# Set-up spread over more points, early evictions, pools of their own, last block by halves, in a hybrid decoder step

## The chip, the cores and the metric

The kernel runs on one NeuronCore of a Trainium2 chip. The metric is device microseconds of one execution, taken as the median of the runs. In profile rows PE is the matmul engine (PEld its weight loads), DVE the vector engine, ACT the scalar engine, POOL the GpSimd engine and SP the queue that issues most transfers. PSUM is the accumulator memory that PE writes, SBUF the working memory.

## What is computed

One step of a two-layer decoder trunk in float32 on 512 prompt tokens and 64 sample tokens (8 sequences of 8), model width 1024, feed-forward width 2816. Layer 0 mixes tokens by dilated attention (three groups, 8 heads of 64), layer 1 by a complex diagonal state-space model (64 groups of 16 channels, 64 states each). Each is followed by a SwiGLU feed-forward.

```python
def attention_layer(h, pos, bufs, w_qkv, q_gain, k_gain, w_o):
    qkv = (h @ w_qkv).reshape(B, T, 3, N_DIL, N_HEAD_SLOTS, HEAD_DIM)
    q = rope(rmsnorm(qkv[:, :, 0], q_gain), pos)
    k = rope(rmsnorm(qkv[:, :, 1], k_gain), pos)
...
    return o @ w_o, new_bufs

def ssm_layer(h, state0, w_in, a_re, a_im, log_dt, b_re, b_im, c_re, c_im, d_skip, w_glu):
    u = (h @ w_in)
    dt = jnp.exp(log_dt)[:, None]
    abar = jnp.exp(lam * dt)
    bbar = ((abar - 1.0) / lam)[..., None] * bmat
...

def swiglu(h, w_gate, w_up, w_down):
    return (jax.nn.silu(h @ w_gate) * (h @ w_up)) @ w_down

def trunk(x, pos, attn_bufs, ssm_states, p):
    for i in range(DEPTH):
        h = rmsnorm(x, p['norm_mix'][i])
...
        x = x + out
        x = x + swiglu(rmsnorm(x, p['norm_ffn'][i]), ...)
```

Besides the two outputs it returns the new key and value caches and the new state.

## The kernel before

The program runs through the phases in order: `qkv_phase`, `attn_phase`, `wo_phase` (attention's output product and residual), `ffn` of layer 0, `ssm_phase`, `ffn` of layer 1. From `wo_phase` on, all activations lie transposed, feature by token, in `xT` (8 tiles of 128 features by NT = 576 tokens, two halves of HN = 288). A tile framework inserts the semaphores and orders the instructions of each engine by its own estimate, except those that are kept in program order (`Kept`, `tc.keep_in_program_order`) or held behind another with `tc.issue_after`. A tile from a pool waits until the last user of its buffer is done; a pool that closes gives its memory to later pools, whose first users then wait for the last users of the old one.

Every large product takes both operands as a high and a low part and adds three products: `split_w` makes the parts of a weight load (512 KB `raw` from HBM, ACT copies `whi`, DVE subtracts for `wlo`, each with two buffers), `split` those of an activation, and `mm6` issues six matmuls of 288 columns.

**QKV.** `qkv_chunk` makes 512 columns of Q, K or V at a time, nine chunks (`CHUNKS`), each in four quarters `kk` of the contraction over five row tiles `t` of tokens, in five PSUM buffers. Between the quarters a queue of slots runs score products, rotations and transposes of earlier chunks; the order is kept. After the chunk `qk_chunk` or the V variant empties the accumulators on ACT into tiles `a`; the next chunk starts in the buffer of `t = 0`.

**Attention and output.** `attn_phase` writes its result to `att`. In `wo_phase`, `ath` is the high part of `att` (ACT), `atl` the low part (DVE); `xr0` to `xr3` are the quarters of the residual, loaded back from HBM and added to the products by DVE. Three accumulators `acc0` to `acc2`, two banks each, are used in turn; the first of them lie on the banks of attention.

**Feed-forward and set-up.** `ffn` goes over the inner width in three parts (`THIRDS`). For each 256 columns there are two weight loads for the gate and two for the up product, 48 matmuls for each load (four contraction tiles, two 128-wide row tiles `m`, six matmuls); the down product follows in four blocks `c`. DVE multiplies the gate accumulator (`gt`), ACT takes silu, POOL multiplies, DVE makes `ut` with the up accumulator and the split of the result (`hh`, `hl`). In layer 0 a generator, `ssm_setup`, is advanced by `step()` after each inner tile and each down block, 34 times; it computes the constants of the state-space layer. Its last loop runs over eight rounds `f`: DVE makes the products `wr`, PE transposes them into `aux`, ACT copies them to `wo`; DVE fills `cb` from `Cr` and `Cn`, PE multiplies `wr` by `cb`, DVE copies to `kk`, PE transposes `kk`, DVE copies that to `kt`, spreads it with eight shuffles into `st` and masks it (stored as T); POOL makes six products for V, in the buffers of `wr` and `wt`. In layer 1 the last third's blocks are transposed back by PE (`aux`), copied by ACT to `yo` and by DVE to `ys`, and stored (`o_yp` from SP, `o_ys` from ACT).

Of the kernel before, what the change touches and what calls it, by code (L numbers as in the profile page):

```python
# [50 lines left out]
def _build(nc, tc, A, es):  # L51
# [50 lines left out]

    def mm6(ps, wh, wl, xh, xl, first, last):
        for i, (w, x) in enumerate(((wh, xh), (wh, xl), (wl, xh))):
            for c in range(2):
                te.matmul(ps[:, c, :HN], w, x[:, c * HN:(c + 1) * HN], start=first and i == 0, stop=last and i == 2)  # L106
# [16 lines left out]
    with ExitStack() as qs:  # L123
# [24 lines left out]
        rs_.close()  # L148
# [4 lines left out]
    accp = es.enter_context(tc.tile_pool(name="acc2", bufs=1, space=PSUM))  # L153
    turn = [0]

    def acc(i=None):
        if i is None:
            i = turn[0] % 3
            turn[0] += 1
        return accp.tile([128, 2, 512], F32, name=f"acc{i}")  # L160
# [261 lines left out]
def qkv_phase(nc, tc, A, es, L):  # L422
# [233 lines left out]
    def v_chunk(gi, wk, vt=None, order=range(5), then=None):  # L656
# [93 lines left out]
def attn_phase(nc, tc, A, es, L):  # L750
# [7 lines left out]
    kp = es.enter_context(pool("kpa", bufs=4))  # L758
# [169 lines left out]
    values(15, dec[7].out)  # L928
    return wo, raws[1]


def wo_phase(nc, tc, A, es, L):
    v, s, g, te = nc.vector, nc.scalar, nc.gpsimd, nc.tensor
    pool, xT, att, fetch_w, split_w, mm6, acc, n0 = (L[x] for x in ("pool", "xT", "att", "fetch_w", "split_w", "mm6", "acc", "n0"))
    wk = es.enter_context(pool("wko"))
    xr = []
    for c in range(4):
        xr.append(wk.tile([128, 2, NT], F32, name=f"xr{c}"))
        nc.sync.dma_start(xr[c], L["xscr"][:, 2 * c:2 * c + 2])
    ath = wk.tile([128, 4, NT], F32R, name="ath")  # L940
    atl = wk.tile([128, 4, NT], F32R, name="atl")
    kv_, ks = Kept(tc, v), Kept(tc, s)
    for k in range(4):
        ks.activation(ath[:, k], att[:, k], AF.Copy)
# [24 lines left out]
    return last  # L969
# [5 lines left out]
def ffn(nc, tc, A, L, layer, nin, nout, fill):  # L975
# [4 lines left out]
    def step():  # L980
# [3 lines left out]
    def gemm(src, width, ks, c0, xs, first=True, last=True):  # L984
        ps = [acc() for _ in range(2)]
        for a in range(0, len(ks), 4):
            n = min(4, len(ks) - a)
            wh, wl = load_w(src, width, ks[a], n, c0, 256)
            for m in range(2):
                for k in range(n):  # L990
                    xh, xl = xs[ks[a + k]]
                    mm6(ps[m], wh[:, k, m * 128:(m + 1) * 128], wl[:, k, m * 128:(m + 1) * 128], xh, xl, a + k == 0, a + k == len(ks) - 1)
        return ps

    with ExitStack() as es:
        hp = es.enter_context(pool("hp", bufs=9))
        wk = es.enter_context(pool("wkf", bufs=2))
        for c0, c1 in THIRDS:
            h = {}
            for c in range(c0, c1):  # L1000
# [9 lines left out]
                for m in range(2):  # L1010
# [3 lines left out]
                    step()  # L1014
# [555 lines left out]
```

## Time and profile before

| | before |
|---|---|
| median of 3 runs | 1504.01 us (1503.43 to 1505.36) |
| profiled execution | 1506.59 us |
| its span, granted clock | 1504.8 us, 0.999 |
| PE / DVE / ACT / POOL busy | 98% / 60% / 35% / 21% |

The span is the time between the first and last instruction of the profiled execution. A row of the timeline gives start and duration in microseconds, engine, line, operation, output and inputs, shape and count; in brackets stands the idle time of that engine just before and what ended it. A row of the waits gives who waited for whom: total, times and longest. A row of a group gives the line, what it does, its count, busy time, mean nanoseconds of one and idle time ahead. In a row by windows, busy microseconds and counts of PE, PEld, DVE, ACT and POOL follow the length of the window.

### The profile page before, as it was taken

The page shows a single profiled execution, that of the slowest core. Times are in us where ns is not written, and L with a number is a line of the kernel's source. Part 1 is how long each engine was busy: PE and PEld are TensorE (multiplying, and loading weights), DVE is VectorE, ACT ScalarE, POOL GpSimd, SP SyncE. Part 2 cuts the span into 40 slices and gives each one's busy share as a digit, 9 for nine tenths or more (in the row PEclk, how much of TensorE's full clock was granted, in tenths as well). Part 3 has the DMA queues.
Part 4 walks back from the last instruction along what each step waited for, and adds up shares of the span by engine and source line. Part 5 has one row for each costly group of instructions (what it writes and reads, how often), then busy time and mean ns, then how long its engine had stood idle before and what let it go on. Part 6 is the DMA issues. An engine that isn't in the chain of part 4 may idle for free. (4 is left out here: it accounts for less than half of the span.)

```text
span 1504.8 us, 29545 instructions
## 1 busy us (share of the span) xinstructions
PE 1471.7 (98%) x12406; PEld 1382.3 (92%) x12406; DVE 909.9 (60%) x1507; ACT 526.1 (35%) x814; POOL 322.3 (21%) x377
## 2 busy tenths in 40 slices
PE   9999999999899999999999999999999999999998
PEld 7878777777799999999999999899999999999998
DVE  5898988745468653789778568745443333333332
ACT  4534455464552222222122454433432222221222
POOL 2022231320040138345345220211111001100100
PEclk9999999999999999999999999999999999999999
DMA  7566788989875555987667748864555555442212
GB/s 245 208 228 234 236 287 264 359 299 348 243 240 196 196 198 183 310 275 256 238 215 260 280 124 254 251 218 157 194 196 195 222 194 195 137 137 84 84 64 71
DMA packets 191253, 322.64 MB, mean 214 GB/s; under 512 B 39984, under 2 KB 137520, under 8 KB 189712
## 3 DMA queue, kind: packets, MB, share of 16 engines
q1 hardware_dynamic: 182960, 303.24, 59.5%
q10 hardware_dynamic: 4992, 10.04, 2.0%
q0 software_dynamic: 3168, 7.48, 1.4%
q8 instruction: 97, 1.59, 0.4%
q14 instruction: 36, 0.29, 0.1%
HBM read 289.22 MB, written 118.78 MB: 271 GB/s over the span
## 5 line engine op out<-in xcount | busy, mean ns | idle before, releaser
L106 PE MATMUL acc<-xgl,whi 128*128 128x288 f32 x1760 | 379.3, 296 | 1.0 <-DVE xgl L173 1.0
L106 PE MATMUL acc<-xgh,wlo 128*128 128x288 f32 x1760 | 377.3, 295 | 0.0
L106 PE MATMUL acc<-xgh,whi 128*128 128x288 f32 x1760 | 377.2, 296 | 0.1
L100 DVE TENSOR_TENSOR wlo<-raw,whi 128x1024 fp32r<-128x1024 f32 (+1 forms) x166 | 205.3, 1237 | 238.6 <-ACT whi L99 235.4
L99 ACT ACTIVATE whi<-raw 128x1024 fp32r<-128x1024 f32 (+1 forms) x166 | 172.4, 1039 | 461.1 <-PE acc L106 409.6
L106 PEld LDWEIGHTS acc<-xgl,whi 128*128 128x128 f32 x1760 | 282.7, 188 | 2.5 <-DVE xgl L173 1.3
L106 PEld LDWEIGHTS acc<-xgh,wlo 128*128 128x128 f32 x1760 | 283.0, 188 | 0.6 <-issue 0.2
L106 PEld LDWEIGHTS acc<-xgh,whi 128*128 128x128 f32 x1760 | 281.6, 188 | 0.5 <-DVE gt L1005 0.3
L1007 POOL TENSOR_TENSOR gt<-gt,rstd 128x576 f32<-128x576 f32 x44 | 77.2, 1756 | 430.6 <-ACT gt L1006 430.5
L106 PE MATMUL acc<-hh,whi 128*128 128x288 f32 x704 | 151.3, 296 | 0.0
L106 PE MATMUL acc<-hh,wlo 128*128 128x288 f32 x704 | 151.3, 295 | 0.0
L106 PE MATMUL acc<-hl,whi 128*128 128x288 f32 x704 | 151.0, 295 | 0.0
L338 PE MATMUL acc<-whi,xh 128*128 128x512 f32 x288 | 118.9, 414 | 3.7 <-ACT a L747 2.0
L106 PEld LDWEIGHTS acc<-hl,whi 128*128 128x128 f32 x704 | 113.1, 188 | 0.2 <-issue 0.2
L106 PEld LDWEIGHTS acc<-hh,wlo 128*128 128x128 f32 x704 | 113.1, 188 | 0.2 <-issue 0.2
L106 PEld LDWEIGHTS acc<-hh,whi 128*128 128x128 f32 x704 | 113.1, 188 | 0.0
L338 PE MATMUL acc<-wlo,xh 128*128 128x512 f32 x288 | 112.2, 391 | 0.0
L338 PE MATMUL acc<-whi,xl 128*128 128x512 f32 x288 | 111.5, 393 | 0.0
L193 POOL TENSOR_TENSOR ssum<-ssum,sq 128x576 f32<-128x576 f32 x21 | 36.2, 1723 | 159.2 <-ACT sq L192 159.2
L338 PEld LDWEIGHTS acc<-whi,xh 128*128 128x128 f32 x288 | 54.0, 188 | 14.5 <-ACT a L747 2.7
L1019 DVE TENSOR_TENSOR xT<-acc,xT 128x576 f32<-128x576 f32 x48 | 36.3, 757 | 49.2 <-PE acc L106 49.2
L1006 ACT ACTIVATE gt<-gt 128x576 f32<-128x576 f32 x44 | 30.2, 686 | 100.2 <-DVE gt L1005 94.5
(389 smaller groups left out, 2047.5 us busy)
## 6 DMA issues: line engine op xcount, KB each, us to landing
o_kv_s<-cache_kv_w SPq DMA_DIRECT2D x64, 1020.0 KB, 7.1
kc<-cache_kv_w SPq DMA_DIRECT2D x100, 512.0 KB, 7.1
raw<-ffn_w_gate SPq DMA_DIRECT2D x44, 512.0 KB, 3.9
raw<-ffn_w_up SPq DMA_DIRECT2D x44, 512.0 KB, 3.8
raw<-ffn_w_down SPq DMA_DIRECT2D x40, 512.0 KB, 3.5
raw<-w_qkv SPq DMA_DIRECT2D x36, 512.0 KB, 7.0
kc<-qscr SPq DMA_DIRECT2D x32, 512.0 KB, 6.2
o_kv_s<-cache_kv_w SPq DMA_DIRECT2D x16, 1008.0 KB, 5.8
```

Source lines behind the costliest of these rows:

```text
L99: s.activation(hi, raw, AF.Copy)
L100: mark[0] = v.tensor_tensor(lo, raw, hi.bitcast(F32), OP.subtract)
L106: te.matmul(ps[:, c, :HN], w, x[:, c * HN:(c + 1) * HN], start=first and i == 0, stop=last and i == 2)
L193: g.tensor_tensor(self.ss, self.ss, sq, OP.add)
L338: ins = nc.tensor.matmul(*a, **kw)
L1006: s.activation(t, t, AF.Silu)
L1007: g.tensor_tensor(t, t, nin.r, OP.mult)
L1019: v.tensor_tensor(xv, ps[m][:, :, :HN], xv, OP.add)
```

## The change

All five parts keep the arithmetic; PE has the same matmuls, and one more store is issued each from ACT and from SP. The changed kernel's file is longer, so its line numbers are higher.

**1. Projections.** The accumulators of row tiles 0 and 1 of every chunk but the first are emptied right after their last matmul, inside the chunk's last quarter:

```diff
-        ps = qkv_chunk(nc, L, x, begin, step, x.prep if first else None, None if first else slot)
-        at = [wk.tile([128, 512], F32, name="a", bufs=6) for _ in range(5)]
-        for t in range(4):
-            s.activation(at[t], ps[t], AF.Copy, scale=x.rc[:, t:t + 1])
+        def ends(ps, t):
+            if t < 2:
+                at.append(wk.tile([128, 512], F32, name="a", bufs=6))
+                s.activation(at[t], ps[t], AF.Copy, scale=x.rc[:, t:t + 1])
+
+        ps = qkv_chunk(nc, L, x, begin, step, x.prep if first else None, None if first else slot, range(5), None if first else ends)
...
-            ps = qkv_chunk(nc, L, x, begin, step, None, slot)
-            for t in range(5):
+            ps = qkv_chunk(nc, L, x, begin, step, None, slot, range(5), lambda ps, t: ends(ps, t) if t < 2 else None)
+            for t in range(2, 5):
```

ACT's rows at the end of the last chunk of K, before (`kT` and `ks` are copies of transposes, `Sall` of scores, `a<-acc` the evictions):

```order
L747 ACTIVATE kT_94<-pt 128x4x128
L747 ACTIVATE ks<-pt 128x512
L747 ACTIVATE Sall<-Sd 128x136
L747 ACTIVATE kT_94<-pt 128x4x128
L747 ACTIVATE Sall<-Sd 128x136
L747 ACTIVATE a<-acc,rr 128x512 x4
L747 ACTIVATE ks<-acc,rr 64x512
L747 ACTIVATE whi<-raw 128x1024
```

and after:

```order
L760 ACTIVATE kT_94<-pt 128x4x128
L760 ACTIVATE Sall<-Sd 128x136
L760 ACTIVATE a<-acc,rr 128x512
L760 ACTIVATE ks<-pt 128x512
L760 ACTIVATE a<-acc,rr 128x512
L760 ACTIVATE kT_94<-pt 128x4x128
L760 ACTIVATE ks<-pt 128x512
L760 ACTIVATE Sall<-Sd 128x136
L760 ACTIVATE kT_94<-pt 128x4x128
L760 ACTIVATE Sall<-Sd 128x136
L760 ACTIVATE a<-acc,rr 128x512 x2
L760 ACTIVATE ks<-acc,rr 64x512
```

Two of the four evictions moved ahead of the chunk's last copies of `ks`, `kT` and `Sall`.

**2. Attention's output.** `ath` gets a pool of its own on the other side of memory and is filled in `attn_phase`, its rows 0 to 2 ahead of the last products; the products of the first block are reordered, so that row 3 comes last. The three accumulators get PSUM pools of their own.

```diff
     dec[7].values(1)
-    values(15, dec[7].out)
-    return wo, raws[1]
+    ek.close()
+    ath = L["rs_"].enter_context(L["right"]("wath")).tile([128, 4, NT], F32R, name="ath")
+
+    def between():
+        dec[7].out()
+        for k in range(3):
+            s.activation(ath[:, k], att[:, k], AF.Copy)
+
+    values(15, between)
+    s.activation(ath[:, 3], att[:, 3], AF.Copy)
+    return wo, raws[1], ath
...
-                for m, k in ((m, k) for m in range(2) for k in range(4)) if x is atl else ((m, k) for k in range(4) for m in range(2)):
+                for m, k in ((0, 0), (0, 1), (0, 2), (1, 0), (1, 1), (1, 2), (0, 3), (1, 3)) if x is ath else ((m, k) for m in range(2) for k in range(4)):
...
-    accp = es.enter_context(tc.tile_pool(name="acc2", bufs=1, space=PSUM))
+    accp = [es.enter_context(tc.tile_pool(name=f"acc2{i}", bufs=1, space=PSUM)) for i in range(3)]
```

**3. Residual quarters.** Each quarter has a pool of its own and its load is kept in program order; the ten small loads of `ssm_setup` are held behind the last of them.

```diff
-        xr.append(wk.tile([128, 2, NT], F32, name=f"xr{c}"))
-        nc.sync.dma_start(xr[c], L["xscr"][:, 2 * c:2 * c + 2])
+        xr.append(es.enter_context(pool(f"wko{c}")).tile([128, 2, NT], F32, name=f"xr{c}"))
+        xl = tc.keep_in_program_order(nc.sync.dma_start(xr[c], L["xscr"][:, 2 * c:2 * c + 2]))
...
-        nc.sync.dma_start(tmask, A["c_tm"])
+        with tc.issue_after(L["xload"].ins):
+            nc.sync.dma_start(tmask, A["c_tm"])
```

SP's queue from the weight load ahead of them, before:

```order
L87 DMA raw<-ffn_w_gate 128x4x256
L1120 DMA raw<-ssm_a_re 32x128
L1121 DMA raw<-ssm_a_im 32x128
L1123 DMA ldt<-ssm_log_dt 32x2
L1127 DMA cw<-ssm_c_re 128x8x64
L1128 DMA cw<-ssm_c_im 128x8x64
L1130 DMA bw<-ssm_b_re 128x32x16
L1131 DMA bw<-ssm_b_im 128x32x16
L939 DMA xr_5039<-x_scr 128x1152
L939 DMA xr_5041<-x_scr 128x1152
L939 DMA xr_5043<-x_scr 128x1152
L939 DMA xr_5045<-x_scr 128x1152
```

and after:

```order
L87 DMA raw<-ffn_w_gate 128x4x256
L961 DMA xr_5049<-x_scr 128x1152
L961 DMA xr_5054<-x_scr 128x1152
L961 DMA xr_5059<-x_scr 128x1152
L961 DMA xr_5064<-x_scr 128x1152
L1110 DMA tmask<-c_tm 128x8
L1113 DMA dcol<-ssm_d 128x8x1
L1117 DMA dmask<-c_dm 128x16
L1159 DMA raw<-ssm_a_re 32x128
L1161 DMA raw<-ssm_a_im 32x128
L1164 DMA ldt<-ssm_log_dt 32x2
L1169 DMA cw<-ssm_c_re 128x8x64
```

The four `xr` loads moved ahead of seven loads of the set-up; the three others (`tmask`, `dcol`, `dmask`) followed them before and still do, and all of `cw` and `bw` follow.

**4. The set-up.** `tick()` takes the place of `step()`, after every weight load's matmuls (68 times instead of 34), and the generator has about twice as many yields. A round of its last loop now takes four ticks: transposes of `wr`; products; transpose of `kk`, shuffles and `powers(f + 1)`, which are DVE's products and `cb` copies of the next round; mask and V. PE's part is held behind the last matmul so far, and V is made in the buffer `st`.

```diff
+            tick()
         return ps
...
+            def powers(f):
...
+                wr[f] = wk.tile([128, 2, 4, 16, 8], F32, name="wr")
+                wt = wk.tile([128, 2, 4, 16, 8], F32, name="wt")
+                cmul(v, wr[f][:, 0], wr[f][:, 1], bw_(Br), bw_(Bi), rv(Ar), rv(Ai), wt[:, 0], wt[:, 1])
                 for i, c in ((0, Cr), (1, Cn)):
                     for gl in range(2):
                         hs = slice(gl * 64, gl * 64 + 64)
                         v.tensor_copy(cb[i][hs, :, gl, :], c[hs, qs, :])
+
+            powers(0)
+            yield
+            yield
+            for f in range(8):
+                ps = aux.tile([128, 2, 512], F32, name="aux")
+                with tc.issue_after(L["pem"][0].ins):
...
+                s.activation(wo.rearrange("p r q c -> p r (q c)"), ps, AF.Copy)
+                nc.sync.dma_start(scn["W"][f], wo)
+                yield
+                pk = aux.tile([128, 2, 512], F32, name="aux")
+                with tc.issue_after(L["pem"][0].ins):
...
+                v.tensor_copy(kk, pk[:, 0, :128])
+                v.scalar_tensor_tensor(k7, dmask, dcol[:, f:f + 1], k7, op0=OP.mult, op1=OP.add)
+                yield
+                with tc.issue_after(L["pem"][0].ins):
+                    te.transpose(pk[:, 1, :128], kk, ident)
+                kt = wk.tile([128, 128], F32, name="kk")
+                v.tensor_copy(kt, pk[:, 1, :128])
...
+                if f < 7:
+                    powers(f + 1)
+                yield
...
+                vv = wk.tile([128, 8, 128], F32, name="st").rearrange("p (r q) (c t) -> p r q c t", r=2, c=16)
+                vt_ = wk.tile([128, 4, 16, 8], F32, name="vt")
```

DVE's rows in one round, from the `cb` copies beside the products on, before (`wlo` is a weight split, `gt<-acc` an eviction of a gate accumulator, `wo<-st` the mask):

```order
L1264 COPY cb_7374<-Cr 64x4x16 x2
L1271 COPY kk<-aux 128x128
L1264 COPY cb_7375<-Cn 64x4x16 x2
L1273 SCALAR_TENSOR_TENSOR kk<-dmask,dcol,kk 128x16
L100 TENSOR_TENSOR wlo<-raw,whi 128x1024
L1276 COPY kt<-aux 128x128
L1285 STREAM_SHUFFLE st<-kt 128x128 x8
L1005 TENSOR_TENSOR gt<-acc_7417,rstd 128x576
L1286 TENSOR_TENSOR wo<-st,tmask 128x8x128
L1086 TENSOR_TENSOR wt<-Br,Ar 128x512
L1087 TENSOR_TENSOR wt<-Bi,Ai 128x512
L1005 TENSOR_TENSOR gt<-acc_7418,rstd 128x576
```

and in a round after, where the second form of `kk<-aux` is the copy of the transpose (`hl` is an activation's low part):

```order
L1335 COPY kk<-aux 128x128
L1126 TENSOR_TENSOR wr<-wt 128x512
L1312 COPY cb_7458<-Cn 64x4x16 x2
L100 TENSOR_TENSOR wlo<-raw,whi 128x1024
L1337 SCALAR_TENSOR_TENSOR kk<-dmask,dcol,kk 128x16
L174 TENSOR_TENSOR hl<-ut,hh 128x576
L1127 TENSOR_TENSOR wt<-Br,Ai 128x512
L1128 TENSOR_TENSOR wt<-Bi,Ar 128x512
L1129 TENSOR_TENSOR wr<-wt 128x512
L1124 TENSOR_TENSOR wt<-Br,Ar 128x512
L1125 TENSOR_TENSOR wt<-Bi,Ai 128x512
L1342 COPY kk<-aux 128x128
```

Two rows for `wr` and four for `wt` moved from behind the mask to between the copy to `kk` and the copy of its transpose, and so did a weight split and an activation's split; after the last row shown follow another weight split and the shuffles.

**5. Last block.** For the last 256 columns of the output both weight loads come first, then all 36 matmuls of `m = 0` and all of `m = 1`; the second half is transposed in the third accumulator, and each half has tiles and stores of its own, 128 wide.

```diff
+                if done and c == 3:
+                    ps = [acc() for _ in range(3)]
+                    ws = [load_w(lw("ffn_w_down"), D, k, min(4, 2 * c1 - k), c * 256, 256) for k in ks[::4]]
...
+                    pt = ps[2] if c == 3 and m else aux.tile([128, 2, 512], F32, name="aux")
...
+                    if m or c == 3:
+                        cc = c * 256 + (m * 128 if c == 3 else 0)
+                        nc.sync.dma_start(dram(A["o_yp"], cc, [[D, 128], [128 * D, 4], [1, w]]), yo)
+                        nc.scalar.dma_start(dram(A["o_ys"], cc, [[D, 64], [1, w]]), ys)
```

More of the change, by code (lines that the diff above doesn't have):

```diff
@@ L105, in mm6 @@
             for c in range(2):
-                te.matmul(ps[:, c, :HN], w, x[:, c * HN:(c + 1) * HN], start=first and i == 0, stop=last and i == 2)
+                pem[0] = te.matmul(ps[:, c, :HN], w, x[:, c * HN:(c + 1) * HN], start=first and i == 0, stop=last and i == 2)
     def newton(y, t, m, v=v):
@@ L159, in acc @@
             turn[0] += 1
-        return accp.tile([128, 2, 512], F32, name=f"acc{i}")
+        return accp[i].tile([128, 2, 512], F32, name=f"acc{i}")
     aux = es.enter_context(tc.tile_pool(name="aux2", bufs=1, space=PSUM))
@@ L968, in wo_phase @@
             n0.add(2 * c + m)
-    return last
+    return last, xl
 THIRDS = ((0, 4), (4, 8), (8, 11))
@@ L1013, in ffn @@
                     h[2 * c + m] = L["split"](hp, t.rearrange("p a b -> p (a b)"), None, "hh", "hl")
-                    step()
             for c in range(4):
-                ps = gemm(lw("ffn_w_down"), D, range(2 * c0, 2 * c1), c * 256, h)
+                ks = range(2 * c0, 2 * c1)
+                done = c1 == 11 and nout is None
+                if done and c == 3:
+                    ps = [acc() for _ in range(3)]
+                    ws = [load_w(lw("ffn_w_down"), D, k, min(4, 2 * c1 - k), c * 256, 256) for k in ks[::4]]
+                else:
+                    ps, ws = gemm(lw("ffn_w_down"), D, ks, c * 256, h), None
                 for m in range(2):
+                    if ws is not None:
+                        for a, k in enumerate(ks):
+                            wh, wl = (w[:, a % 4, m * 128:(m + 1) * 128] for w in ws[a // 4])
+                            mm6(ps[m], wh, wl, *h[k], a == 0, k == ks[-1])
                     xv = xT[:, 2 * c + m, :].rearrange("p (a b) -> p a b", a=2)
@@ L1264, in ssm_setup @@
                         v.tensor_copy(cb[i][hs, :, gl, :], c[hs, qs, :])
-                pk = aux.tile([128, 2, 512], F32, name="aux")
-                for i in range(2):
-                    for q in range(4):
-                        te.matmul(pk[q * 32:q * 32 + 32, 0, :128], cb[i][:, q].rearrange("p a b -> p (a b)"), wr[:, i, q].rearrange("p c s -> p (c s)"),
-                                  start=i == 0, stop=i == 1, tile_position=(0, q * 32), skip_group_check=True)
+            powers(0)
+            yield
+            yield
+            for f in range(8):
+                qs = slice(f * 4, f * 4 + 4)
+                ps = aux.tile([128, 2, 512], F32, name="aux")
+                with tc.issue_after(L["pem"][0].ins):
+                    for ri in range(2):
+                        for q in range(4):
+                            te.transpose(ps[:, ri, q * 128:(q + 1) * 128], wr[f][:, ri, q].rearrange("p c s -> p (c s)"), ident)
+                wo = wk.tile([128, 2, 4, 128], F32, name="wo")
+                s.activation(wo.rearrange("p r q c -> p r (q c)"), ps, AF.Copy)
+                nc.sync.dma_start(scn["W"][f], wo)
+                yield
+                pk = aux.tile([128, 2, 512], F32, name="aux")
+                with tc.issue_after(L["pem"][0].ins):
+                    for i in range(2):
+                        for q in range(4):
+                            te.matmul(pk[q * 32:q * 32 + 32, 0, :128], cb[i][:, q].rearrange("p a b -> p (a b)"), wr[f][:, i, q].rearrange("p c s -> p (c s)"),
+                                      start=i == 0, stop=i == 1, tile_position=(0, q * 32), skip_group_check=True)
                 kk = wk.tile([128, 128], F32, name="kk")
@@ L1273, in ssm_setup @@
                 v.scalar_tensor_tensor(k7, dmask, dcol[:, f:f + 1], k7, op0=OP.mult, op1=OP.add)
[L1274 to L1275 removed]
+                yield
+                with tc.issue_after(L["pem"][0].ins):
+                    te.transpose(pk[:, 1, :128], kk, ident)
+                kt = wk.tile([128, 128], F32, name="kk")
                 v.tensor_copy(kt, pk[:, 1, :128])
[L1277 to L1278 removed]
                 st = wk.tile([128, 8, 128], F32, name="st")
```

105 lines of the change are left out of this document (56 added, 49 removed).

## The prediction

> **What bounds the kernel now.** I read the head of the page first, then the waits of the matmul engine over the span, then the timeline around each of them.
>
> ```profile
> span 1504.8 us, 29545 instructions
> PE 1471.7 (98%) x12406; PEld 1382.3 (92%) x12406; DVE 909.9 (60%) x1507; ACT 526.1 (35%) x814; POOL 322.3 (21%) x377
> ```
>
> PE is busy for 98% of the span, so the end moves only where PE waits. The change leaves out no matmul. What it can win is bounded by PE's idle time, 1504.8 − 1471.7 = 33.1 us, and what it can lose lies in new waits. The waits by releaser (total, times, longest, all in us) that lie in places the change touches:
>
> ```profile
> PE aux L1274 <- DVE kk L1273: 4.7, 7, 0.7
> PE acc L338 <- ACT a L747: 3.0, 3, 1.0
> PE acc L106 <- DVE xT L967: 1.7, 1, 1.7
> PE acc L957 <- ACT ath L747: 1.4, 1, 1.4
> PE aux L1028 <- DVE ys L1031: 1.3, 1, 1.3
> PE aux L1257 <- DVE wr L1091: 1.3, 1, 1.3
> PE aux L1268 <- ACT wo L1259: 0.8, 2, 0.6
> PE Sd L576 <- ACT ks L747: 0.7, 1, 0.7
> ```
>
> The first seven make 4.7 + 3.0 + 1.7 + 1.4 + 1.3 + 1.3 + 0.8 = 14.2 us: the most that the change can bring, one term for each of its parts. I take them in the order of the program.
>
> **1. Early evictions in the projections: 3.0 us.** The start of a chunk of QKV columns, from the timeline:
>
> ```profile
> 270.45 2.42 ACT L747 ACTIVATE a<-acc,rr 128x512 f32<-128x512 f32 x4
> 271.19 0.50 PE L338 MATMUL acc<-whi,xsp 128*128 128x512 f32 x1 [1.01 <-ACT a L747]
> ```
>
> ACT empties four accumulators one after another, 0.60 us each, only when the whole chunk is done; PE needs the first at once and waits 1.0. Three of the eight later chunks show it. For the pitch of the matmuls, a stretch of ten microseconds without a wait (PE busy and count come first):
>
> ```profile
> 766.00:776.00 10.00, 10.00 (x78) 10.00 (x77) 10.00 (x24) 2.44 (x3) 4.43 (x3) 1.00 0.70 245
> ```
>
> 10.0 / 78 is 0.13 us for 288 columns, and so 0.23 for 512.
> With the change rows 0 and 1 are emptied during the last quarter of the chunk, in front of some ACT copies of other work. Row 2's bank is needed only 24 matmuls into the next chunk, and 24 × 0.23 is 5.5 us, while ACT reaches it within 1.2. So no wait takes the place of these. The price: two copies of 0.60 us stand ahead of the `ks` and `kT` copies. The nearest row is the last one of the list above, PE waiting 0.7 for `ks`; three such would cost 2.1. I take 0, since other matmuls stand between those copies and the score products; the range for the term is 0.9 to 3.0.
>
> **2. Attention's high part and the residual quarters: 1.3 + 1.7 us.** Timeline around the output projection:
>
> ```profile
> 397.73 1.58 PE L747 MATMUL O<-P,vt 128*32 128x128 f32 x49
> 399.43 2.41 ACT L747 ACTIVATE ath<-att 128x576 fp32r<-128x576 f32 x4 [0.84 <-PE O L747]
> 399.45 1.10 DVE L747 TENSOR_TENSOR att<-att,O 128x512 f32<-128x512 f32 x1 [1.37 <-PE O L747]
> 400.70 0.50 PE L957 MATMUL acc<-ath,whi 128*128 128x288 f32 x2 [1.39 <-ACT ath L747]
> 404.75 3.57 SPq L939 DMA_DIRECT2D xr<-x_scr  x4
> 410.83 1.08 DVE L966 TENSOR_TENSOR xT<-acc,xr 128x288 f32<-128x288 f32 x2 [6.49 <-DMA xr<-x_scr]
> 412.19 0.50 PE L106 MATMUL acc<-ath,whi 128*128 128x288 f32 x2 [1.70 <-DVE xT L967]
> ```
>
> Before, the `ath` tile lies on memory of the attention phase, so ACT starts it only after the last O matmul. With room of its own, rows 0 to 2 are copied before that. Row 3 needs DVE's product (end 400.55) and takes 0.6; PE reaches it after 24 matmuls × 0.13 = 3.1 us from 399.4, at 402.5. The second row tile's accumulator sits on O's bank, free at 400.55; PE reaches it after 12 matmuls, at 401.0. So nearly all of the 1.39 goes: 1.3 (bounds 0.7, if that bank is late, and 1.4).
>
> The residual: SP issues `xr` at 404.75, behind the state-space set-up's small loads, and the first quarter lands at 410.8, 6 us after. The change puts the quarters ahead of those loads on SP; their memory is free when the last O matmul and ACT's last copy before it are done, by 399.4. Even with 6 us to land, data are there by 405.5, and the first accumulators are complete at about 407.5. The adds (1.08 + 0.22, about 1.2) then end near 409, and PE needs the bank at 412.19 − 1.70 − 1.3 = 409.2. So the whole 1.7 goes (bounds 1.2 and 1.7). The set-up's ten small loads are issued after `xr` instead, some 8 us later, and PE uses none of them before the feed-forward.
>
> **3. Set-up spread over more points: 4.8 of 6.8 us.** `ssm_setup` feeds PE with eight rounds of transposes and small products inside the feed-forward's matmuls. Its three waits sum to 4.7 + 1.3 + 0.8. Before, a round's products and the transpose of their result `kk` stand half a weight load apart:
>
> ```profile
> 647.30 0.39 DVE L1264 COPY cb<-Cr 64x64 f32<-64x64 f32 x2 [0.38 <-PE aux L1268]
> 647.72 0.29 DVE L1271 COPY kk<-aux 128x128 f32<-128x128 f32 x1
> 648.04 2.31 DVE L1264 COPY cb<-Cn 64x64 f32<-64x64 f32 x2
> 650.38 1.20 DVE L1273 SCALAR_TENSOR_TENSOR kk<-dmask,dcol,kk 128x16 f32<-128x16 f32 x1
> 651.50 1.21 DVE L100 TENSOR_TENSOR wlo<-raw,whi 128x1024 fp32r<-128x1024 f32 x1
> ```
>
> DVE needs 651.5 − 647.3 = 4.2 us for the chain from product to `kk`; 25 matmuls × 0.13 are 3.3. Hence 0.7 each time. Afterwards a whole weight load, 48 × 0.13 = 6.3 us, stands between them, and 6.3 as well between the transposes of `wr` and the products that wait for ACT's copy of them (1.0 us). These seven and two waits go. So does the 1.3 for `wr`, computed half a round earlier.
>
> What is late next is DVE. Between PE's products of a round and the second weight split after them (which PE needs two weight loads on), the new order puts the products `powers(f+1)`. The groups of DVE in these 250 us (busy, mean ns):
>
> ```profile
> L100 DVE TENSOR_TENSOR wlo<-raw,whi 128x1024 fp32r<-128x1024 f32 (+1 forms) x37 | 46.7, 1262 | 10.5 <-ACT whi L99 10.3
> L1264 DVE COPY cb<-Cn 64x64 f32<-64x64 f32 x16 | 16.4, 1025 | 0.3
> L1086 DVE TENSOR_TENSOR wt<-Br,Ar 128x512 f32<-128x512 f32 x8 | 14.6, 1828 | 0.0
> L173 DVE TENSOR_TENSOR hl<-ut,hh 128x576 fp32r<-128x576 f32 x14 | 10.6, 756 | 5.4 <-ACT hh L172 5.4
> L1087 DVE TENSOR_TENSOR wt<-Bi,Ai 128x512 f32<-128x512 f32 x8 | 8.8, 1104 | 0.0
> L1091 DVE TENSOR_TENSOR wr<-wt 128x512 f32<-128x512 f32 x8 | 5.5, 692 | 0.3
> L1264 DVE COPY cb<-Cr 64x64 f32<-64x64 f32 x16 | 3.0, 189 | 12.9 <-PE aux L1268 12.8
> ```
>
> The chain is: one 128x576 product 0.75, `cb` 0.4, `kk` 0.3, `wr` 0.7, `cb` 2.0 to 2.3, split 1.25, `kk` 1.2, `hl` 0.75, two products 2.2, `wr` 0.7, two products 2.2 (2.9 with the 1828 ns mean), copy of the transposed `kk` 0.3, split 1.25: 14.0 to 15.0. Neighbours overlap by some 0.07 us (650.38 + 1.20 against a next start at 651.50), over 16 pieces 1.1, so 12.9 to 13.9. PE gets there after its own products 0.75, 6.3, the transpose 0.33, 6.3 and the four matmuls that use the high part alone, 0.5: 14.2. Between 0.3 and 1.3 us to spare, with single operations in these rows that take twice their time. Next, the eviction of a gate accumulator follows 1.7 us of shuffles (eight at a start-to-start distance of 0.2) and 0.7 after that: 15.3 to 16.3, needed 24 matmuls after 13.7, at 16.9. So a part of the rounds will miss by a few tenths. I put 2.0 us for all eight (0.25 each) and keep 6.8 − 2.0 = 4.8. Bounds: 6.8 if none misses, 0 if each of the seven misses by 1.0.
>
> Other covers here hold. The shuffles now write the buffer from which the previous round's V is stored; POOL makes V in six operations, of which these are the shortest and nearly the longest form:
>
> ```profile
> L1296 POOL TENSOR_TENSOR wt<-Cr,Ai 128x512 f32<-128x512 f32 x8 | 16.8, 2102 | 0.6
> L1294 POOL TENSOR_TENSOR wr<-wr,wt 128x512 f32<-128x512 f32 x8 | 10.3, 1282 | 0.0
> ```
>
> Six of them make 8 to 13 us, and a round is 4 × 6.3 us and PE's own products long, 27 us. The early part (transposes of C beside the long exponential chain on DVE) keeps two buffers, each refilled a weight load of 3 us or more ahead.
>
> On `cb`: the same 64x64 copy takes 189 ns from `Cr` and 1025 from `Cn`, where POOL works on V. [...]
>
> **4. Last block by halves: 0.4 us.** The end of the program:
>
> ```profile
> 1497.99 0.60 ACT L1030 ACTIVATE yo<-aux 128x512 f32<-128x512 f32 x1 [3.28 <-DVE xT L1019]
> 1498.61 0.28 DVE L1031 COPY ys<-aux 64x128 f32<-64x128 f32 x1 [0.76 <-ACT yo L1030]
> 1498.95 0.66 PE L1028 MATMUL aux<-ident,xT 128*128 128x128 f32 x4 [1.34 <-DVE ys L1031]
> 1499.76 0.60 ACT L1030 ACTIVATE yo<-aux 128x512 f32<-128x512 f32 x1 [1.17 <-PE aux L1029]
> 1500.70 0.47 ACTq L1033 DMA_DIRECT2D o_ys<-ys  x1
> o_ys<-ys ACTq DMA_DIRECT2D x4, 64.0 KB, 3.0
> ```
>
> A bank of its own lets the second half's transposes start at 1497.9 instead of 1498.95. But ACT now issues the first half's `o_ys` between its two copies: it waits for DVE's `ys` at 1498.9 and takes 0.47, so the second copy starts near 1499.4 instead of 1499.76. That keeps 0.4 of PE's 1.3. The end is set by `o_ys`, 3.0 us to land at 64 KB; I take it that half the size lands no sooner. Bounds: 0 and PE's whole 1.3. I take 0.4.
>
> **Sum.** 3.0 + 1.3 + 1.7 + 4.8 + 0.4 = 11.2 us. The profiled execution took 1506.6 (span 1504.8) and would take 1495.4; it stands 2.6 above the median of the runs, 1504.0, which would become 1492.8.
>
> **Rivals.** (a) DVE takes the set-up's gain back: each of seven rounds misses its weight split by 1.0. For it speaks the thin margin, against it that before the change DVE idled where it waited for PE's products (12.8 us in the `cb` row), which the spread fills. Then 6.4 is left: 1497.6. (b) The early evictions move a wait to `ks` (2.1) and the tail gives nothing: 11.2 − 2.5 gives 1495.3. (c) Slower: the DVE chain runs against POOL in every round. V now starts after the round's last DVE product and runs into the next round's chain; if all six POOL operations fall there and each costs DVE the 1025 − 189 = 0.84 us of the `cb` rows, three more than my chain holds, it is 2.5 us longer, and late by some 2 in the rounds with little margin; with a gate eviction behind it, about 2.8 in each of the six rounds that lie in gate and up products: −16.8 against 13.2 won (the 6.4 and the 6.8), so 1507.6. It decides from 2.2 us per round on.
>
> **Chances.** A measurement of this kernel tells 0.2%, 3.0 us, from no change. My sum, with a range of its own from all bounds at their best to 9 us won (1489.8 to 1495.0), 0.55; (a) 0.20; (b) 0.10; (c) at full strength 0.08, and so strong that it about cancels the gain 0.07. Faster 0.85, same 0.07, slower 0.08. The range goes from all bounds at their best (3.0 + 1.4 + 1.7 + 6.8 + 1.3 = 14.2: 1489.8), less the 0.6 by which the fastest run shown lies under the median, to 1500, which takes in (a) and a part of its worse side.
>
> **What would show it.** In the new profile the rows for `a`, `ath`, `xT <- xr`, `kk` and `wr` leave PE's waits, `xr` is issued before 400, and the second `yo` copy starts about 0.4 us after the first `o_ys` issue began. Wrong in part 3: PE waits for `wlo` or for the eviction `gt` in 600 to 830 us, once a round. Wrong in part 1: more waits for `ks`, `kT` or `att` before 290 us. Wrong altogether: the feed-forward stretch of 430 to 830 us isn't shorter.

## The result, and the profile after

The changed kernel takes 1498.79 us (median of 13 runs, 1494.86 to 1506.64), the kernel before on the same chip 1506.26 (13 runs, 1502.65 to 1512.33). The ratio is 0.9947 (95% interval 0.9933 to 0.9961): some 8.0 us faster, between 5.9 and 10.1. The forecast was 11.2 us won and 1492.8 us. The profiled execution took 1499.43 us. Head of its page:

```profile
span 1497.7 us, 29564 instructions
PE 1472.2 (98%) x12406; PEld 1384.5 (92%) x12406; DVE 895.8 (60%) x1507; ACT 527.8 (35%) x814; POOL 323.1 (22%) x377
```

PE's idle time fell from 33.1 us to 1497.7 − 1472.2 = 25.5. Of PE's waits the rows for accumulators that wait for `a`, and those for `ath`, `xT` of the residual, `kk`, `wr` and `wo` are gone. These rows (total, times, longest) stand in their place or were small before:

```profile
PE acc L108 <- DVE wlo L100: 4.3, 2, 2.2
...
PE Sd L578 <- ACT ks L760: 2.2, 2, 1.6
...
PE pt L566 <- DMA kc<-cache_kv_w: 1.3, 1, 1.3
```

`ks` was 0.7 in one wait before. Two new waits for a weight split, `wlo`, cost 4.3.

To place gains and losses I compared when PE starts the same matmul in the two profiled executions. The changed kernel is ahead by 0.4 us at 21 us, 1.0 at 100, 1.1 at 303, 0.8 at 398, 2.2 at 404, 4.1 at 410 and at 590, 6.7 at 865 to 937, 6.0 at 990, 5.7 at 1471 and 7.2 at the end. The first 0.4 is chance: two executions of one and the same program up to 400 us stood 1.9 apart at 21 us. The next 0.6 belongs to part 1: transposes of `a` waited for DVE three times before, and once after, as the waits show (before, then after).

```profile
PE pt L642 <- DVE a L747: 1.2, 3, 0.7
```
```profile
PE pt L655 <- DVE a L760: 0.6, 1, 0.6
```

The two that went stood at 83 and 98 us. From 21 to 100 us PE takes 79.2 us in each of the eight executions here that have part 1, and 79.8 in each of the five that don't.

| term | predicted, us | measured, us | from |
|---|---|---|---|
| 1. early evictions | 3.0 | 0.7 in this pair; 1.8 as a mean | 21 to 303 us, experiments below |
| 2. `ath` | 1.3 | 1.4 | 398 to 404 us |
| 2. residual quarters | 1.7 | 1.9 | 404 to 410 us |
| 3. set-up | 4.8 | 2.6 | 410 to 865 us |
| 4. last block | 0.4 | 1.5; 1.1 in late_oldtail, below | 1471 us to the end |

With the mean for the first term and 1.5 for the last the sum is 9.2. Between 937 and 1471 us, where no part of the change lies, the pair lost 1.0. The runs give 8.0.

**Output projection**, timeline after:

```profile
397.59 1.85 ACT L760 ACTIVATE ath<-att 128x576 fp32r<-128x576 f32 x3
398.45 0.53 PE L978 MATMUL acc<-ath,whi 128*128 128x288 f32 x2
398.59 1.97 SPq L961 DMA_DIRECT2D xr<-x_scr  x4
399.82 0.69 ACT L760 ACTIVATE ath<-att 128x576 fp32r<-128x576 f32 x1 [0.37 <-DVE att L760]
404.60 1.14 DVE L987 TENSOR_TENSOR xT<-acc,xr 128x288 f32<-128x288 f32 x2 [1.01 <-PE acc L978]
```

ACT begins the first three rows of `ath` while PE still works on attention, and PE's first product has no wait in brackets. The quarters are issued at 398.59 instead of 404.75, and DVE's addition waits for PE, no longer for the load.

**Set-up.** No weight split was late within a round. One link of the forecast's chain was wrong in the safe direction, as the groups of DVE from 590 to 850 us show (the mean of one, in ns, is the second number after the bar):

```profile
L1312 DVE COPY cb<-Cr 64x64 f32<-64x64 f32 x16 | 4.4, 274 | 0.1
L1312 DVE COPY cb<-Cn 64x64 f32<-64x64 f32 x16 | 3.0, 186 | 0.1
```

The copies from `Cn` took 1025 ns each before (939 to 1358 beside V on POOL in fourteen of the sixteen, 186 and 191 in the two with POOL idle) and 186 now, with none beside POOL. So DVE's chain is shorter than I worked out. The smallest slack of a weight split in the rounds between 600 and 835 us was 2.0 us, where I had 0.3 to 1.3. What did come late are the two ends. The first, timelines of POOL, SP, DVE and PE after, and the issue of the store (KB, us to landing):

```profile
577.49 0.74 POOL L1129 TENSOR_TENSOR ee<-et,et 128x256 f32<-128x256 f32 x1
```
```profile
578.25 0.68 SPq L1291 DMA_DIRECT2D e_scr<-ee  x1
```
```profile
e_scr<-ee SPq DMA_DIRECT2D x1, 2048.0 KB, 9.3
```
```profile
587.72 0.31 DVE L1298 MEMSET cb<- 128x128 f32 x2 [4.62 <-DMA e_scr<-ee]
587.94 0.97 DVE L1124 TENSOR_TENSOR wt<-Br,Ar 128x512 f32<-128x512 f32 x1
...
594.67 0.69 DVE L1129 TENSOR_TENSOR wr<-wt 128x512 f32<-128x512 f32 x1
595.28 1.22 DVE L100 TENSOR_TENSOR wlo<-raw,whi 128x1024 fp32r<-128x1024 f32 x1
```
```profile
596.56 0.53 PE L108 MATMUL acc<-xgh,wlo 128*128 128x288 f32 x2 [2.24 <-DVE wlo L100]
```

POOL's products for E end at 578.2; the 2 MB store of E takes 9.3 us; `cb` lies on E's memory, so DVE stands still until 587.7. Then the first round's products, `powers(0)`, stand in DVE's order in one piece of 7.3 us ahead of the split that PE needs at 594.3.

The second end, DVE, POOL and PE:

```profile
839.48 2.25 DVE L1354 TENSOR_TENSOR wo<-st,tmask 128x1024 f32<-128x1024 f32 x1
...
843.69 4.92 DVE L179 SCALAR_TENSOR_TENSOR xgl<-xT,gm,xgh 128x576 fp32r<-128x576 f32 x2
848.47 2.43 DVE L100 TENSOR_TENSOR wlo<-raw,whi 128x1024 fp32r<-128x1024 f32 x1
```
```profile
844.97 2.40 POOL L1363 TENSOR_TENSOR st<-st,vt 128x512 f32<-128x512 f32 x1
```
```profile
850.95 0.53 PE L108 MATMUL acc<-hh,wlo 128*128 128x288 f32 x2 [2.10 <-DVE wlo L100]
```

The last round's V runs on POOL while DVE already makes `xgl` for the next phase; a single `xgl` takes 2.46 us there and 0.82 at 406.97 us. Both ends together give back 4.3 of the 6.8 us.

That 6.8 − 4.3 comes so near the measured 2.6 is in part chance, since two more amounts cancel. PE's time from 410 to 865 us less its waits is 450.8 us before and 450.9 in oldsetup (below), and 448.7 to 449.8 in the six executions of new set-ups whose granted clock stayed at 1.00 there: the waits that went cost 1 to 2 us more than their rows say. Most of that stands at the eight transposes of `kk`: from the start of the matmul before to the start of the one behind, with the wait left out, PE took 0.38 us at the seven that waited and 0.17 at the eighth, and takes 0.16 at each now. Against it the granted clock was 0.91 from 590 to 610 us, behind the first new wait (last section), and the changed kernel stands at 450.7.

**Last block**, timeline and issues after:

```profile
1492.93 0.47 ACTq L1069 DMA_DIRECT2D o_ys<-ys  x1
1493.53 0.60 ACT L1064 ACTIVATE yo<-acc 128x512 f32<-128x512 f32 x1 [0.94 <-PE acc L1063]
...
1494.47 0.47 ACTq L1069 DMA_DIRECT2D o_ys<-ys  x1
```
```profile
o_ys<-ys ACTq DMA_DIRECT2D x1, 64.0 KB, 3.0
o_ys<-ys ACTq DMA_DIRECT2D x2, 32.0 KB, 2.2
```

The last store lands 2.2 us after its issue, where 64 KB take 3.0.

### The profile page after: what moved, and what is told of

Its sections match the earlier page's. It is cut to its first block, busy times and chain, and to the rows that moved or that the text cites. A ratio compares the mean times of both kernels' runs of the same rounds, so it can differ in the third digit from the quotient of the medians.

```text
span 1497.7 us, 29564 instructions
## 1 busy us (share of the span) xinstructions
PE 1472.2 (98%) x12406; PEld 1384.5 (92%) x12406; DVE 895.8 (60%) x1507; ACT 527.8 (35%) x814; POOL 323.1 (22%) x377
## 5 line engine op out<-in xcount | busy, mean ns | idle before, releaser
L100 DVE TENSOR_TENSOR wlo<-raw,whi 128x1024 fp32r<-128x1024 f32 (+1 forms) x166 | 214.9, 1295 | 261.9 <-ACT whi L99 258.4
L1029 POOL TENSOR_TENSOR gt<-gt,rstd 128x576 f32<-128x576 f32 x44 | 72.9, 1659 | 489.3 <-ACT gt L1028 489.1
L340 PEld LDWEIGHTS acc<-whi,xl 128*128 128x128 f32 x288 | 54.0, 188 | 12.0
L340 PEld LDWEIGHTS acc<-whi,xh 128*128 128x128 f32 x288 | 54.0, 188 | 11.2 <-ACT xh L280 0.9
```

Of the source, the lines that this page charges most:

```text
L100: mark[0] = v.tensor_tensor(lo, raw, hi.bitcast(F32), OP.subtract)
L340: ins = nc.tensor.matmul(*a, **kw)
L1029: g.tensor_tensor(t, t, nin.r, OP.mult)
```

## The experiments

Each kernel is the changed one with the edit shown; a time is the median beside the kernel before on the same chip. Where the time differs by a few us between executions of the same program, I read PE's position between fixed matmuls instead.

### Parts 1 and 5 undone (late_oldtail)

```diff
-        ps = qkv_chunk(..., range(5), None if first else ends)
+        ps = qkv_chunk(...)
+        ends(ps, 0)
+        ends(ps, 1)
...
-                if done and c == 3:
-                    ps = [acc() for _ in range(3)]
...
+                ps, ws = gemm(lw("ffn_w_down"), D, ks, c * 256, h), None
```

> The changed kernel with part 1 (early evictions) and part 5 (last block by halves) undone. Theory T (transfers set the pace of the projections up to about 205 us): the three waits for `a` (3.0 us) come back, the waits for `ks` fall from 2.2 to about 0.7 and the one for `kc` (1.3) goes, so the output projection starts at most 0.9 us later than in the changed kernel; the tail costs 1.4 more, from the last matmul's bank to the end. Together 1.5 to 2.5 us slower than the changed kernel. Rival (the sizes of the prediction): 3.0 for part 1 and 0.4 for part 5, 3.4 slower, of which nearly all before 300 us.

1501.85 us, ratio 0.9958 (0.9942 to 0.9974). The three waits for `a` (3.0) are back, and those for `ks` and, but for 0.2, for `kc` are gone. From 1481 us to the end it loses 1.1 us on the changed kernel: the halves of the last block. The other 0.3 of the 1.5 above stays won with part 5 undone, and its cause stays open. At 310 us PE was 0.8 behind the changed kernel, and at 182 us, before the first of the three waits, already 0.95, of which 0.6 arose between 21 and 100 us: where the three waits came back, the early evictions had won nothing in that pair. By the ratios the whole is some 1.7 us slower than the changed kernel, within the 1.5 to 2.5 of theory T, but the intervals overlap.

### Fewer rows for a broadcast load (light, late_light)

The broadcast of Q for the sample scores, `kc <- qscr`, on 64 of its 128 partitions, and DVE's product with it, with and without part 1; half of those scores are left out. It was meant to make the loads lighter.

```diff
-            kept(nc.sync.dma_start(qb, dram(qscr, ..., [[0, 128], [512, 2], [1, 512]])))
+            kept(nc.sync.dma_start(qb[:64], dram(qscr, ..., [[0, 64], [512, 2], [1, 512]])))
```

> The changed kernel with the broadcast loads `kc <- qscr` on 64 of 128 partitions (256 KB instead of 512), so that half of the third group's sample scores is left out. Theory T: the loads behind them land earlier, the wait for `kc` (1.3) goes and the waits for `ks` fall from 2.2 to under 1.0, and PE is 1.5 to 2.5 us earlier at 300 us than in the changed kernel. Rival Q (the early copies on ACT hold up the `ks` copies behind them): the waits for `ks` stay at about 2 us, with fewer bytes too.

> Part 1 undone and the broadcast loads halved as in `light`. Theory T: with transfers out of the way the evictions are worth their full wait: three waits for `a` of 1.0, no wait for `kc`, and PE 2 to 3 us later at 300 us than in `light`. Rival Q: the `ks` waits are small here (0.7) and the difference to `light` is at most 1 us.

1503.93 us (0.9974, 0.9954 to 0.9994) and 1503.76 (0.9977, 0.9957 to 0.9997), neither as good as the changed kernel's 0.9947. The premise failed. Windows of 100 to 200 us (the last two columns are the DMA share and GB/s), the changed kernel and then light:

```profile
100.00:200.00 100.00, 96.47 (x587) 77.35 (x586) 88.44 (x116) 44.87 (x73) 20.79 (x48) 1.00 0.77 268
```
```profile
100.00:200.00 100.00, 96.81 (x587) 77.48 (x586) 88.62 (x116) 45.06 (x73) 20.51 (x50) 1.00 0.81 229
```

Fewer bytes per us, and the DMA engines were busier with them. In light PE's waits for `kc` grew to 3.8 and for `ks` to 2.6. That agrees with loads that set the pace, but it doesn't test it. Of the sizes expected the opposite came: between the fixed matmuls named below light needs 208.8 us and late_light 205.3, so with slower loads the early evictions lost 3.5 us. Part of that is the granted clock, 0.91 from 190 to 210 and from 285 to 305 us in light and 1.00 in late_light.

### Every second broadcast load left out (half, late_half)

Whole partitions, and half as many loads; the tile of the part before is used again, so half of the third group's sample scores have another value. With and without part 1.

```diff
-            qb = kst.tile([128, 2, 512], F32, name="kc")
-            kept(nc.sync.dma_start(qb, dram(qscr, ...)))
+            if part % 2 == 0:
+                qbs[b] = kst.tile([128, 2, 512], F32, name="kc")
+                kept(nc.sync.dma_start(qbs[b], dram(qscr, ...)))
+            qb = qbs[b]
```

> The changed kernel with every second broadcast load of the sample scores (kc from the scratch of Q) left out; its tile of the part before is used again, so half of those scores have another value. Theory T (in the stretch of 180 to 240 us the loads set the pace, so early evictions have nothing to win there): with fewer bytes PE's waits for kc (1.3) and for ks (2.2 in 2) go or fall below 0.8 in all, and PE stands 1.5 to 3 us earlier at 300 us than in the changed kernel. Rival Q (ACT's two early copies stand ahead of ks): the ks waits stay at about 2 and PE's position at 300 us moves by less than 1. Whole time 1496 to 1498 by T.

> As half, and the evictions of rows 0 and 1 put back behind the chunk's end (part 1 undone). By T, with the loads out of the way, the evictions are worth what PE waits for a in this kernel: 3.0 in 3 waits, and PE stands 2 to 3 us later at 300 us than in half. By rival Q the early copies only trade the waits: the difference at 300 us is 1 or less.

1497.46 us (0.9926, 0.9902 to 0.995) and 1499.33 (0.9946, 0.9928 to 0.9965). In half no wait for `kc` or `ks` is left, though ACT's two early copies stand where they stood: rival Q falls. PE needs 198.7 us between two fixed matmuls (at 100.2 and 303.1 us in the changed kernel) in half and 202.1 in late_half, whose waits show

```profile
PE acc L340 <- ACT a L762: 3.0, 3, 1.0
```

So the early evictions are worth 3.4 us in this pair of profiles, near what the forecast gave them (3.0), once fewer loads come. The medians lie 1.9 apart, with intervals that overlap.

With all loads whole I have nine executions, six of programs that are the same up to 400 us:

| us between fixed matmuls | 182 to 204 | 204 to 303 | 100 to 303 |
|---|---|---|---|
| part 1 kept: mean of 6 (lowest to highest) | 20.8 (19.3 to 22.2) | 99.4 (98.9 to 99.9) | 202.1 (200.2 to 204.1) |
| part 1 undone: mean of 3 | 20.3 (19.8 to 20.8) | 101.0 (100.7 to 101.3) | 203.3 (202.8 to 204.1) |
| half / late_half | 18.3 / 19.5 | 98.4 / 100.7 | 198.7 / 202.1 |

The two waits behind 204 us give 1.6 of their 2.0. The one at 190 us gives nothing, since a load decides there. With the 0.6 before 100 us the mean of the term is 1.8. In the two longest of the six (nolastv 203.3, oldsetup 204.1, both below) a wait for `ks` of 2.1 and 2.3 us was followed by a granted clock of 0.91 from 190 to 210 us; in the other four it was 1.00. Timelines after, SP, DVE, ACT, PE:

```profile
185.57 0.34 SPq L523 DMA_DIRECT2D kc<-qscr  x1
```
```profile
194.24 1.23 DVE L760 TENSOR_TENSOR kc<-kc 128x1024 f32<-128x1024 f32 x1 [3.53 <-DMA kc<-qscr]
```
```profile
197.88 0.58 ACT L760 ACTIVATE ks<-pt 128x512 f32<-128x512 f32 x1
```
```profile
188.77 0.63 PE L566 MATMUL pt<-ident,kc 128*128 128x128 f32 x4 [1.28 <-DMA kc<-cache_kv_w]
198.51 0.43 PE L578 MATMUL Sd<-ks,Qz 128*32 128x128 f32 x8 [1.63 <-ACT ks L760]
```

The broadcast issued at 185.57 holds DVE until 194.24; DVE's reductions behind it hold ACT's third `t <- a`, and `ks` stands behind that on ACT. In the kernel before, the broadcast was issued at 186.59, and let DVE go at the same time. PE starts the same product at the same time too, and waits less only because it came there later. DVE and PE before:

```profile
194.24 1.23 DVE L747 TENSOR_TENSOR kc<-kc 128x1024 f32<-128x1024 f32 x1 [2.15 <-DMA kc<-qscr]
```
```profile
198.51 0.43 PE L576 MATMUL Sd<-ks,Qz 128*32 128x128 f32 x8 [0.70 <-ACT ks L747]
```

### Part 4 undone (oldsetup)

The old generator and `step()`, the other parts kept.

```diff
-    def tick():
+    def step():
...
-            powers(0)
-            yield
-            yield
-            for f in range(8):
+            for f in range(8):
+                cmul(v, wr[:, 0], wr[:, 1], ...)
```

> The changed kernel with part 4 undone: the set-up of before, at the points of before (its small loads still behind the residual's). Theory: seven waits for `kk` (4.7), one for `wr` (1.3), two for `wo` (0.8) come back and the two waits for `wlo` (4.3) go, so the stretch from the first gate product to the next norm is 2.5 us longer (2 to 3). Rival, the prediction's term: 4.8 longer.

1501.73 us, ratio 0.996 (0.9944 to 0.9976). PE's waits:

```profile
PE aux L1320 <- DVE kk L1319: 4.7, 7, 0.7
...
PE aux L1303 <- DVE wr L1130: 1.3, 1, 1.3
```

Those of before, and no `wlo`. PE's position against the changed kernel moves by 2.5 us between 430 and 911 us, the 2.6 of the pair above: the set-up's part is worth 2.5 to 2.6, not 4.8.

### Last V left out (nolastv)

The six products of V of the eighth round on POOL are left out, so that eighth of V has another value.

```diff
+                if f < 7:
                     g.tensor_tensor(vv[:, 0], cb_(Cr), p1r, OP.mult)
```

> The changed kernel without the six products of V of the last round on POOL (that eighth of V has another value). Theory P (DVE's two products xgl beside POOL's V, 2.46 us each instead of 0.82, bring the wait at 851 us): xgl falls to 1.4 us or less each and the wait at 851 us goes or falls under 0.7; the wait at 596 us stays 2.2. Rival (the mask that waits for its store, and the order of DVE's instructions, are enough): the wait at 851 us stays above 1.5. Whole time 1.5 to 2 us less by P, under 0.7 less by the rival.

1496.90 us, ratio 0.9926 (0.9901 to 0.9951). DVE at the second end:

```profile
838.49 2.25 DVE L1354 TENSOR_TENSOR wo<-st,tmask 128x1024 f32<-128x1024 f32 x1
...
841.85 2.68 DVE L179 SCALAR_TENSOR_TENSOR xgl<-xT,gm,xgh 128x576 fp32r<-128x576 f32 x2
```

`xgl` takes 1.34 us each, the wait at 851 us is gone, and PE gains 2.4 us there on the changed kernel; the mask takes its 2.25 as before, and the wait at 597 us stays (2.40). So the second wait is POOL's V beside DVE's `xgl`. By the ratios the kernel is 3.2 us faster than the changed one, more than the 1.5 to 2 expected; its granted clock stayed at 1.00 behind the first wait (last section).

### Rounds four ticks earlier (gap2)

```diff
-                yield
-                yield
+                if k >= 3:
+                    yield
+                    yield
...
+            yield
+            yield
         with ExitStack() as e2:
             wk = e2.enter_context(pool("ssd", bufs=1))
```

> The changed kernel with six pauses fewer in the set-up's early part and two more between the store of E and powers(0), so that the eight rounds start some four ticks, 25 us, earlier. Theory (the two waits of PE for wlo, 2.2 at 596 us and 2.1 at 851 us, come from the ends of the set-up: the first from the store of E that lands only 9 us after its issue and holds the memory of cb, the second from the last round's mask and V on top of the next phase's normalisation): both go, 4.3 us less, whole time near 1494.5. Rival (the rounds themselves are too full and the waits would come to another round): wlo waits of 2 or more stay somewhere in 560 to 860 us and the time falls by less than 2.

1494.77 us, ratio 0.9915 (0.9884 to 0.9946). The second wait is gone, the first is not:

```profile
594.07 0.85 PE L108 MATMUL acc<-xgh,wlo 128*128 128x288 f32 x2 [2.18 <-DVE wlo L100]
```

My reason for the first was half wrong. The store of E went at 575.83, no earlier relative to PE: what times it is POOL's chain of products for E, 43 us from 535 to 578, of which POOL is busy for 39.9, in the changed kernel, not the number of ticks. `powers(0)` stood in the same place of DVE's order. The time came near the 1494.5 expected though one of the two waits stood, so not by the mechanism named.

### powers(0) in two pieces (gap3), and without part 1 (late_gap3)

```diff
-            powers(0)
-            yield
-            yield
+            powers(0, 1)
+            yield
...
+            with tc.issue_after(L["mark"][0].ins):
+                powers(0, 2)
+            yield
```

`mark` is the latest weight split. Run beside the changed kernel itself (after2).

> The changed kernel once more, on the chip of the two that follow. All theories: PE's waits for wlo are again 2.2 near 596 us and 2.1 near 851 us; time about 0.995 of before.

> As gap2, but powers(0) is cut in two: the real part of the products is issued three ticks after the store of E, the imaginary part and the copies to cb a few ticks later and held behind the weight split that comes between. Theory D (the wait at 596 us comes from DVE's order: eight operations of powers(0), 7.5 us, stand in one piece ahead of the weight split after the store of E has landed): the split ends at about 590.5, 3.8 us after the first memset of cb, PE needs it near 592, and no wlo wait over 0.5 is left; 4.3 us less than the changed kernel, 2 less than gap2. Rival (the store of E and its landing late are what counts, whatever the order behind them): a wait of 1.5 or more stays at 590 to 600 us, for wlo or for gt.

> gap3 with part 1 undone (rows 0 and 1 emptied behind the chunk's end). Theory T (loads of the sample scores set the pace where two of the three a waits stand): the whole time is 0.3 to 1.3 us above gap3's, and the three a waits of 3.0 are back. If the early evictions were worth what I predicted of them it would be 2.5 to 3.5 above; if they cost what they win, 0.3 or less.

1500.39 us (0.9959, 0.9943 to 0.9975), 1493.70 (0.9916, 0.9901 to 0.993) and 1495.60 (0.9925, 0.9912 to 0.9938). gap3 is 6.7 us under the changed kernel beside it, but its ratio is that of gap2 (0.9915), not the 2 us less that I expected. Its DVE, POOL and PE:

```profile
589.72 1.76 DVE L1313 TENSOR_TENSOR wr<-wt 128x512 f32<-128x512 f32 x1
591.40 1.21 DVE L100 TENSOR_TENSOR wlo<-raw,whi 128x1024 fp32r<-128x1024 f32 x1
...
597.80 2.35 DVE L1312 TENSOR_TENSOR wt<-Bi,Ai 128x512 f32<-128x512 f32 x1
```
```profile
596.97 2.21 POOL L1029 TENSOR_TENSOR gt<-gt,rstd 128x576 f32<-128x576 f32 x1 [6.04 <-ACT gt L1028]
```
```profile
602.01 0.53 PE L108 MATMUL acc<-xgh,wlo 128*128 128x288 f32 x2 [1.48 <-DVE wlo L100]
```

The split comes ahead of the second piece, and the wait at 597 us is gone: DVE's order was its cause. But the work behind the late store is only put off. The pushed-back piece and the first products of `powers(1)` then hold the next split, and 1.5 us are lost one weight load later, outside the 590 to 600 us that I had named. One of these products takes 2.35 us beside POOL's product for `gt`; in the changed kernel, with POOL idle, it took 1.07. Only 0.6 of the wait is won. The other gains of gap3 on after2 are the second end (there 0.9 + 0.4 + 0.8 us in three waits, none here) and a granted clock of 1.00 from 590 to 610 us, where after2 has 0.91 (below); its start, 1.9 us earlier by 21 us, is chance.

In late_gap3 the three `a` waits of 3.0 are back. It is 1.9 us above gap3, which the overlapping runs (1493.07 to 1498.45 and 1493.16 to 1499.18) don't settle between my 0.3 to 1.3 and the 2.5 to 3.5 of the forecast. The positions over all executions, 1.8 us up to 303 us, are the better measure. They lie above my range as well, since I had left out the 0.6 before 100 us.

## Why the prediction was right or wrong

- **Early evictions, 3.0: mis-sized.** The waits for `a` went as said. The step that failed is the price put at 0 for `ks`: PE reached those matmuls earlier, but the loads of the sample scores didn't. I had looked for what hides two ACT copies, not for whether the transfers ahead of `ks` keep up. With fewer loads the three waits gave 3.4; with all of them 1.2 on average, varying by some 2 us either way between executions. To these comes 0.6 from two waits before 100 us that the forecast didn't count, so 1.8. Rival (b)'s price for `ks`, 2.1, came true in the profile (2.2), by another road than the copies it named.
- **`ath` and residual, 1.3 and 1.7: right**, 1.4 and 1.9, with the quarters issued before 400 us as named.
- **Set-up, 4.8: mis-sized, and its mechanism wrong.** I took 2.0 off for rounds that miss by a few tenths. None missed: between 600 and 830 us there is no wait for `wlo` or `gt`. I had timed the chain with `cb` rows that ran beside POOL, and the change moved V away from them. What I hadn't looked at is where the generator begins and ends: a store that frees the memory of `cb` late, and a last V that runs into the next phase. They cost 4.3. Nor had I priced what a wait takes beside its row (1 to 2 us in all, won) or the clock behind a new one (about as much, lost). Rivals (a) and (c), each a miss in every round, did not happen. POOL beside DVE, the mechanism of (c), cost PE a wait once, at the end: `xgl` took 2.46 us there against 1.34 without V (nolastv). Within the rounds weight splits beside POOL took up to 2.44 us (at 712.6 us in the changed kernel) where those with POOL idle took 1.23, and PE waited for none.
- **Last block, 0.4: mis-sized.** The earlier second copy came as worked out: from the end of the last addition to `xT` it starts 1.4 us later instead of 1.9. The failed step is "half the size lands no sooner": 2.2 us instead of 3.0. SP's store beside it was halved at the same time (2.4 us instead of 3.2), so the runs don't show what one of them alone would give.

The errors had both signs (−1.2, −2.2, +1.1, and +0.3 for the two that were right), so they cancel in part. The 8.0 won is less than the 9 with which I had bounded my own sum, and 1498.8 lies in the stated range only by its upper part, which was there for rival (a): that rival did not happen, so this is luck. Of the 6.0 us between 1492.8 and 1498.8 some 3 to 4 are the smaller gain; the rest is that the kernel before, too, stood 2.3 higher in the runs beside it (1506.3 against 1504.0).

## What to carry to other kernels

A wait for an eviction is worth its length only if the operands of the work behind it arrive earlier too (the three waits here gave 1.2 us with all loads and 3.4 with half of the broadcasts): follow the loads to the next few products before booking it. When work is spread over many points, price its first and last piece by themselves, since here buffers taken over from the stage before and the start of the next phase collided there (two waits, 4.3 us) and not in the steady rounds (none for `wlo` or `gt`). Time a moved operation by rows without the neighbour that it moves away from (the `Cn` copies, 1025 ns and 186). And a wait of the bounding engine cost more than its row here (1 to 2 us in the old set-up, 1.3 behind the new wait of 2.24): look at the clock and at the starts behind it too.

## What the runs showed of the hardware

**Behind a wait of 2.1 to 2.6 us the granted clock fell to 0.91 in five of nine executions.** Windows just after the first stall, changed kernel and then nolastv, whose wait was longer (2.40 against 2.24):

```profile
600.00:610.00 10.00, 10.00 (x73) 10.00 (x73) 4.35 (x4) 3.20 (x4) 3.69 (x2) 0.95 0.72 252
```
```profile
600.00:610.00 10.00, 10.00 (x77) 10.00 (x77) 5.12 (x6) 4.32 (x6) 3.72 (x2) 1.00 0.93 361
```

From 590 to 610 us the granted clock was 0.91 in five of the nine executions with a wait of about 2 us or more there (after, after2, gap2, late_oldtail, light) and 1.00 in the other four; at 1.5 and 1.6 us (gap3, late_gap3) it stayed 1.00. Between 575 and 625 us the changed kernel lost 1.3 us more than nolastv. In gap2 a wait of 2.71 us was followed by 0.66:

```profile
953.51 0.70 PE L1464 MATMUL aux<-U,Tc 128*128 128x72 f32 x2 [2.71 <-ACT ys L1467]
```
```profile
950.00:970.00 20.00, 17.29 (x95) 17.05 (x93) 15.26 (x28) 7.69 (x17) 9.83 (x14) 0.66 0.54 133
```

PE lost 6.3 us on the changed kernel between 951 and 977 us, of which the wait is 2.7. Why that wait came in this execution stays open. Waits of 1.8 us were followed by a lower clock elsewhere: in late_light one at 948 us was followed by 0.57, with some 5.7 us lost on the changed kernel from 937 to 985 us,

```profile
950.00:970.00 20.00, 19.76 (x123) 19.49 (x124) 16.61 (x32) 8.66 (x25) 1.28 (x4) 0.57 0.72 206
```

and in gap3 and late_half one at 378 us by 0.89 from 375 to 390 us. Why some of these waits are followed by a lower clock and others not stays open. Length does not separate them: of the nine above, the five at 0.91 waited 2.1 to 2.6 us, the four at 1.00 2.4 to 2.6.

**PE was about 2% slower in one piece of 60 us, at a granted clock of 1.00 both times.** Window of 1320 to 1380 us, before and after:

```profile
1320.00:1380.00 60.00, 60.00 (x452) 60.00 (x452) 19.60 (x21) 11.51 (x12) 0.00 (x0) 1.00 0.36 117
```
```profile
1320.00:1380.00 60.00, 60.00 (x463) 60.00 (x462) 20.03 (x21) 11.13 (x12) 0.00 (x0) 1.00 0.35 113
```

Eleven matmuls fewer before; from 1170 to 1232 us it is the other way round (477 before, 468 after), and gap3 has 453 here. It cost 1.3 us in each of the two places and so moved the positions of the pair by as much there and back. Its cause stays open.
